# VectorE in emission order with column sums that give way, and mixing steps of TensorE joined two by two

## The chip, the cores and the metric

The kernel runs on one core of a Trainium2 chip. The metric is the device time of one execution in microseconds, the median of three runs. All engines of the core run side by side: TensorE (PE) multiplies, VectorE (DVE) and ScalarE (ACT) work element by element, GpSimd (POOL) helps, and SyncE (SP) issues nearly all transfers.

## What is computed

Two layers of a mixer over 256 latent and 256 context tokens of width 2048. Each layer norms and modulates its input, projects it with one wide matrix, runs three branches (Fourier mixing, pooling over windows, retention with 8 heads in two directions), projects each branch back, merges them with gates, and projects once more. The core of the reference:

```python
h = rms_norm(x, norm_g[l]) * (1.0 + scale) + shift          # scale, shift, gate: silu(c) @ w_ada[l] + b_ada[l]
proj = h @ w_in                                              # 2048 x 12288
y_f = (fourier_mix(f_x, w_fourier) * silu(f_g)) @ w_up_fourier
y_p = (pool_mix(p_x, w_pool, pool_scale) * silu(p_g)) @ w_up_pool
o = head_rms(retention(rope(q), rope(k), v))                 # both directions, state handed on from the context
y_r = (o * silu(r_g)) @ w_up_ret
merged = g[:, :, 0] * y_f + g[:, :, 1] * y_p + g[:, :, 2] * y_r
x = x + gate * (merged @ w_out)                              # the context likewise, in layer 0
```

In layer 1 the context only gives the retention's keys and values; its other rows are not computed.

## The kernel before

**Products.** Everything is float32. A number is split into a high and a low part, and a product takes three matmuls: high by high (L151), and the two mixed ones (L152, L153). These three lines are called the main products here. The activations are split once; the weights are split as they come.

**The stream.** The weight blocks of both layers form one list of chunks; a chunk is two 128-row tiles of a block. `stream` (L241 to L264) goes through it: for chunk i it splits chunk i+2 (ScalarE copies the high part `whi`, L206; VectorE subtracts it and leaves the low part `wlo`, L207), SyncE loads chunk i+4 (`raw`, 512 KB, L196), then TensorE multiplies chunk i. There are three `whi` and `wlo` buffers and four `raw` ones. A chunk of layer 0 is four units of six 512-column matmuls; one of layer 1 is mostly two such units.

**Background units.** The modulation matrix `w_ada` is also needed as column sums. That work is cut into units (`bg_chunk`, L438 to L473): each loads 512 KB (`bgraw`, two buffers, SyncE) and does four multiply-adds on VectorE into `bga` (L466, L468), or two where only one vector is wanted (gates of layer 1). After chunk i, five chunks in eight take one unit from the queue `bg`.

**Mixing steps.** The branches' small products (rotary embedding, transposes of heads, decays, scores, attention, Fourier, pooling) wait in the queue `mix` (`Steps`, L162 to L182). After each unit of main products the queue is told how many microseconds have passed, and lets out a step when its `after` and the `gap` of the step before are over; in layer 1 the gaps are multiplied by 0.65 from the third block on. Names that come up below: `rope_a` and `rope_b` (L590, L600: rotary embedding of a token tile, first GpSimd, then two VectorE instructions L604 and L605), `heads_T` (L679: transposes L684 of one head, ScalarE copies the result), `decayed` and `state` (L688, L696), `decays_a` (L704: two VectorE and three ScalarE instructions), `scores` (L725: matmuls L732 and a VectorE product L734), `attend` (L736), `norm_b` (L764: a reciprocal L766 and a product L767 on VectorE), `row_scale` (L1073).

**The border to the output projection.** `out_start` (L999) empties both queues before the first chunk of the output projection of a layer; in layer 0 it also splits the 16 merged tiles (`split_merged`, L996: ScalarE L431, VectorE L432). At the very end some weights are split into kept buffers (ScalarE L212, VectorE L213).

**Order.** TensorE runs in the order in which the program emits its instructions (`tc.manual_schedule` for that engine). The order on VectorE, ScalarE, GpSimd and SyncE is set by the compiler's scheduler, which may move an instruction ahead of those emitted earlier.

Of the kernel before, what the change touches and what calls it, by code (L numbers as in the profile page):

```python
# [19 lines left out]
P = 128  # L20
# [23 lines left out]
def hybrid_kernel(ctx: ExitStack, tc: tile.TileContext, a: dict, out: bass.AP):  # L44
# [196 lines left out]
    def stream(blocks):  # L241
# [17 lines left out]
        for i in range(n):  # L259
            prepare(i + 2)  # L260
            ahead(i + 4)
            chunks[i][0].products(chunks[i][1], parts.pop(i))
            if i > 5 and i % 8 in (1, 3, 5, 6, 7) and bg:
                bg.popleft()()  # L264
# [260 lines left out]
    def layer(l):  # L525
# [96 lines left out]
        class Half:  # L622


            def __init__(self, half):
# [3 lines left out]
                self.osb, self.sq = {}, {}  # L629
# [19 lines left out]
            def q_done(self, t, ps):  # L649
                self.q[t] = evac(ps)  # L650
                if t == 3:
                    for t2 in (2, 3):
                        mix.append(lambda t2=t2: rope_a(self.q, t2), gap=1.2, after=2.0)
# [7 lines left out]
            def queue_heads(self):  # L661
# [17 lines left out]
            def heads_T(self, src, tls, dst, hd):  # L679

                n = len(tls) * P
                pt = mx()
                for i, t in enumerate(tls):
                    T.transpose(pt[:, i * P:(i + 1) * P], src[t][:, hd * P:(hd + 1) * P], ident)  # L684
                dst[hd] = g()
                S.copy(dst[hd][:, 0:n], pt[:, 0:n])

            def decayed(self, d):  # L688
                self.kd = []
                for t in range(2):  # L690
# [3 lines left out]
                    self.kd.append(o)  # L694

            def state(self, d):  # L696
                ps = mx()
                for hh in range(4):
                    c = slice(hh * P, (hh + 1) * P)
                    for t in range(2):  # L700
                        T.matmul(ps[:, c], self.kd[t][:, c], self.v[t][:, c], start=t == 0, stop=t == 1)  # L701
# [97 lines left out]
        def merged_T(j, c2):  # L799

            pt = mx()
            for i in range(2):
                for t in tiles:
                    c = (2 * c2 + i) * P
# [414 lines left out]
```

## Time and profile before

| | us |
|---|---|
| median of three runs | 2446.63 (2446.52 to 2446.91) |
| the profiled execution | 2445.55 |
| its span | 2443.8 |
| TensorE busy | 2392.4 (98%) |
| VectorE busy | 1320.6 (54%) |
| ScalarE busy | 870.4 (36%) |
| GpSimd busy | 240.3 (10%) |

The profile is one execution, 1.08 us below the median. It lists how long each engine was busy, what ended each idle time, and, in the timelines, when each instruction began and how long it took. A matmul of 512 columns is shown with 0.39 us but the next one starts 0.23 us later, since they overlap; so times on TensorE are read from start to start. PEclk is the clock granted to TensorE as a share of 2.4 GHz.

### The profile page before, as it was taken

The page shows a single profiled execution, that of the slowest core. Times are in us where ns is not written, and L with a number is a line of the kernel's source. Part 1 is how long each engine was busy: PE and PEld are TensorE (multiplying, and loading weights), DVE is VectorE, ACT ScalarE, POOL GpSimd, SP SyncE. Part 2 cuts the span into 40 slices and gives each one's busy share as a digit, 9 for nine tenths or more (in the row PEclk, how much of TensorE's full clock was granted, in tenths as well). Part 3 has the DMA queues.
Part 4 walks back from the last instruction along what each step waited for, and adds up shares of the span by engine and source line. Part 5 has one row for each costly group of instructions (what it writes and reads, how often), then busy time and mean ns, then how long its engine had stood idle before and what let it go on. Part 6 is the DMA issues. An engine that isn't in the chain of part 4 may idle for free.

```text
span 2443.8 us, 28705 instructions
## 1 busy us (share of the span) xinstructions
PE 2392.4 (98%) x11288; PEld 1967.8 (81%) x11288; DVE 1320.6 (54%) x1656; ACT 870.4 (36%) x1180; POOL 240.3 (10%) x246
## 2 busy tenths in 40 slices
PE   6999999999999999999999999999999999999998
PEld 3678788778888888888888888878889888888886
DVE  4437657768256258644457432653527544545555
ACT  5222332342222232222222322563426444444444
POOL 0000200200000001110011210230302000110100
PEclk9999999999999999999999999999999999999999
DMA  9955424346345336545466343443335666676664
GB/s 338 348 170 173 138 78 148 92 136 213 115 144 187 93 119 210 156 128 169 130 202 215 112 129 112 147 150 103 100 90 146 211 191 180 181 216 183 189 204 146
DMA packets 226471, 396.58 MB, mean 162 GB/s; under 512 B 14032, under 2 KB 55376, under 8 KB 226336
## 3 DMA queue, kind: packets, MB, share of 16 engines
q1 hardware_dynamic: 221088, 379.74, 50.8%
q0 software_dynamic: 5248, 15.01, 2.1%
q8 instruction: 88, 1.44, 0.2%
q14 instruction: 47, 0.39, 0.1%
HBM read 392.60 MB, written 2.10 MB: 162 GB/s over the span
## 4 chain that ended last, share of the span: by engine, by line
PE 81%; issue 8%; DMA 5%; DVE 4%; POOL 1%; ACT 1%; SPq 0%; DVEq 0%; POOLq 0%; ACTq 0%
PE acc L151 25%; PE acc L152 25%; PE acc L153 25%; DVE bga L468 2%; DMA wa<-in_w_ada_dram 2%; DMA bgraw<-in_w_ada_dram 1%; DVE wlo L207 1%; PE mx L323 1%; PE mx L744 1%; PE mx L732 1%; PE mx L747 1%; POOL g L1085 1%; PE mx L701 0%; DMA raw<-in_w_out_dram 0%; PE mx L889 0%
## 5 line engine op out<-in xcount | busy, mean ns | idle before, releaser
L207 DVE TENSOR_TENSOR wlo<-raw,whi 128x1024 fp32r<-128x1024 f32 (+1 forms) x504 | 624.6, 1240 | 824.5 <-ACT whi L206 824.0
L206 ACT ACTIVATE whi<-raw 128x1024 fp32r<-128x1024 f32 (+1 forms) x504 | 529.2, 1050 | 1153.4 <-PE acc L153 553.5
L151 PE MATMUL acc<-whi,hm 128*128 128x512 f32 x1568 | 621.9, 397 | 0.7 <-ACT g L577 0.7
L152 PE MATMUL acc<-wlo,hm 128*128 128x512 f32 x1568 | 611.7, 390 | 2.2 <-DVE wlo L207 2.2
L153 PE MATMUL acc<-whi,hm 128*128 128x512 f32 x1568 | 611.7, 390 | 0.0
L151 PE MATMUL acc<-hm,whi 128*128 128x512 f32 (+1 forms) x1232 | 461.1, 374 | 0.7 <-ACT whi L206 0.7
L153 PE MATMUL acc<-hm,wlo 128*128 128x512 f32 (+1 forms) x1232 | 453.0, 368 | 1.0 <-DVE wlo L207 1.0
L152 PE MATMUL acc<-hm,whi 128*128 128x512 f32 (+1 forms) x1232 | 452.7, 367 | 0.0
L152 PEld LDWEIGHTS acc<-wlo,hm 128*128 128x128 f32 x1568 | 295.1, 188 | 62.7 <-DVE wlo L207 4.1
L153 PEld LDWEIGHTS acc<-whi,hm 128*128 128x128 f32 x1568 | 294.7, 188 | 62.3
L151 PEld LDWEIGHTS acc<-whi,hm 128*128 128x128 f32 x1568 | 295.0, 188 | 61.2 <-ACT g L577 1.1
L468 DVE SCALAR_TENSOR_TENSOR bga<-bgraw,sc,bga 128x512 f32<-128x512 f32 x420 | 311.8, 789 | 53.1 <-DMA bgraw<-in_w_ada_dram 51.5
L151 PEld LDWEIGHTS acc<-hm,whi 128*128 128x128 f32 x1232 | 232.6, 189 | 42.4 <-ACT whi L206 2.2
L153 PEld LDWEIGHTS acc<-hm,wlo 128*128 128x128 f32 x1232 | 232.4, 189 | 40.5 <-DVE wlo L207 2.2
L152 PEld LDWEIGHTS acc<-hm,whi 128*128 128x128 f32 x1232 | 232.6, 189 | 39.4 <-issue 1.4
L852 POOL TENSOR_TENSOR g<-g,g 128x512 f32<-128x512 f32 x32 | 52.7, 1673 | 726.5 <-DVE g L848 726.5
L151 PE MATMUL acc<-g,whi 128*128 128x512 f32 x256 | 99.7, 390 | 0.0
L152 PE MATMUL acc<-g,whi 128*128 128x512 f32 x256 | 99.6, 389 | 0.0
L153 PE MATMUL acc<-g,wlo 128*128 128x512 f32 x256 | 99.6, 389 | 0.0
L597 POOL TENSOR_TENSOR g<-g,g 128x256 f32<-128x256 f32 x32 | 29.6, 954 | 332.4 <-ACT g L577 332.4
L151 PEld LDWEIGHTS acc<-g,whi 128*128 128x128 f32 x256 | 48.1, 188 | 10.1
L152 PEld LDWEIGHTS acc<-g,whi 128*128 128x128 f32 x256 | 48.1, 188 | 10.0
(213 smaller groups left out, 1888.4 us busy)
## 6 DMA issues: line engine op xcount, KB each, us to landing
raw<-in_w_in_dram SPq DMA_DIRECT2D x368, 512.0 KB, 3.7
bgraw<-in_w_ada_dram SPq DMA_DIRECT2D x128, 512.0 KB, 4.3
raw<-in_w_out_dram SPq DMA_DIRECT2D x72, 512.0 KB, 3.6
wa<-in_w_ada_dram SPq DMA_DIRECT2D x128, 256.0 KB, 6.0
raw<-in_w_up_ret_dram SPq DMA_DIRECT2D x32, 512.0 KB, 3.8
raw<-in_w_up_fourier_dram SPq DMA_DIRECT2D x16, 512.0 KB, 3.7
raw<-in_w_up_pool_dram SPq DMA_DIRECT2D x16, 512.0 KB, 4.4
w<-in_w_in_dram SPq DMA_DIRECT2D x8, 512.0 KB, 6.6
```

What stands on the lines that cost most here:

```text
L151: T.matmul(ps, ah, bh, start=first, stop=False)
L152: T.matmul(ps, ah, bl, start=False, stop=False)
L153: at["product"] = T.matmul(ps, al, bh, start=False, stop=last)
L206: S.activation(hi[:, :, 0:w], raw[:, :, 0:w], AF.Copy)
L207: V.tensor_tensor(lo[:, :, 0:w], raw[:, :, 0:w], hi[:, :, 0:w].bitcast(F32), op=ALU.subtract)
L323: T.matmul(ps[32 * g4:32 * g4 + 32, 0:2 * n * P], sc32[:, kt, :], wa[gi, kt // rows][:, kt % rows, :, :].rearrange("p i c -> p (i c)"), st ...
L468: V.scalar_tensor_tensor(accs[ci, v], raw[:, kk, :], s, accs[ci, v], op0=ALU.mult, op1=ALU.add)
L597: G.tensor_tensor(rv[:, :, :, x, :], pv[:, :, :, 1 - x, :], sv[:, :, x, :].unsqueeze(1).to_broadcast([P, 4, 2, 32]), op=ALU.mult)
L732: T.matmul(ps[:, jt * SEQ:(jt + 1) * SEQ], self.kT[hh][:, k0:k0 + P], qs, start=True, stop=True)
L744: T.matmul(o, self.v[2 * s + jt][:, c], at[:, jt * SEQ:(jt + 1) * SEQ], start=jt == 0, stop=jt == 1 and s == 0)
L747: T.matmul(o, self.st[d][:, c], qd[:, d * SEQ:(d + 1) * SEQ], start=False, stop=d == 1)
L852: G.tensor_tensor(merged[d][:, 0:ntok], merged[d][:, 0:ntok], o[:, 0:ntok], op=ALU.add)
```

## The change

Four things change.

1. VectorE too runs in the order of emission while the stream runs (`manual_schedule` around the stream). The other three engines stay with the scheduler.
2. A background unit is taken only when fewer than two mixing steps are queued, and in three chunks of four instead of five in eight.
3. Mixing steps that have TensorE work are emitted two by two with twice the gap: transposes of two heads, both states, the attention of one head with the scores of the next, Fourier channels with positions, two pooled groups, two transposes of merged or output tiles. The two `decayed` steps now stand ahead of `rope_b`, with buffers for each direction, and the gaps after `rope_a` are doubled.
4. In layer 1 the keys' `heads_T` transposes only the latent token tiles (2, 3), not all four.

```diff
-            if i > 5 and i % 8 in (1, 3, 5, 6, 7) and bg:
+            if i > 5 and len(mix.q) < 2 and i % 4 and bg:
                 bg.popleft()()
...
                     for t2 in (2, 3):
-                        mix.append(lambda t2=t2: rope_a(self.k, t2), gap=0.8, after=2.0)
-                    mix.append(lambda: self.decayed(0), gap=1.6)
+                        mix.append(lambda t2=t2: rope_a(self.k, t2), gap=1.6, after=2.0)
+                    for d in range(2):
+                        mix.append(lambda d=d: self.decayed(d), gap=1.6)
                     for t2 in (2, 3):
                         mix.append(lambda t2=t2: rope_b(self.k, t2), gap=1.0)
-                    mix.append(lambda: (self.state(0), self.decayed(1)), gap=1.6)
-                    for hh in range(4):
-                        mix.append(lambda hh=hh: self.heads_T(self.k, (0, 1, 2, 3), self.kT, hh))
-                    mix.append(lambda: self.state(1))
+                    mix.append(lambda: (self.state(0), self.state(1)), gap=3.0)
+                    for hh in (0, 2):
+                        mix.append(lambda hh=hh: self.heads_T(self.k, tiles, self.kT, hh), gap=4.0)
...
-                    for hh in range(4):
-                        mix.append(lambda hh=hh: self.heads_T(self.q, tiles, self.qT, hh))
+                    for hh in (0, 2):
+                        mix.append(lambda hh=hh: self.heads_T(self.q, tiles, self.qT, hh), gap=4.0)
...
-                    if hh < 4:
-                        mix.append(lambda hh=hh: self.scores(hh))
-                    if hh:
-                        mix.append(lambda hh=hh: self.attend(hh - 1))
+                    mix.append(lambda hh=hh: (self.attend(hh - 1) if hh else None, self.scores(hh) if hh < 4 else None), gap=4.0)
...
-            def heads_T(self, src, tls, dst, hd):
+            def heads_T(self, src, tls, dst, h0):
...
-                        k0 = s * SEQ + jt * P
+                        k0 = s * SEQ - tok0 + jt * P
...
-                for n in range(5):
-                    if n < 4:
-                        mix.append(lambda n=n: windows(n))
-                    if n:
-                        mix.append(lambda n=n: pooled(n - 1))
+                for n in range(0, 4, 2):
+                    mix.append(lambda n=n: windows(n))
+                    mix.append(lambda n=n: windows(n + 1))
+                    mix.append(lambda n=n: (pooled(n), pooled(n + 1)), gap=3.0)
...
     run = stream(blocks0 + blocks1)
-    next(run)
-    for t in range(4):
-        halves0[0].v_done(t, v0_acc[t])
-    for i, ps in enumerate(rg_acc):
-        rg_done0(i, ps)
-    for _ in run:
-        pass
+    with tc.manual_schedule(engines={mybir.EngineType.DVE}):
+        next(run)
+        for t in range(4):
+            halves0[0].v_done(t, v0_acc[t])
+        for i, ps in enumerate(rg_acc):
+            rg_done0(i, ps)
+        for _ in run:
+            pass
```

**The order on VectorE around the queries' rotary embedding** (first half of the heads, layer 0). A row gives line, operation, output and inputs; `bga` are column sums, `wlo` the low part of a chunk's weights, and the `g` buffers on L604 and L605 are two token tiles of the queries. Before:

```order
L468 SCALAR_TENSOR_TENSOR bga_396_2206<-bgraw_467_2543,sc_87,bga_396_2206 128x512
L468 SCALAR_TENSOR_TENSOR bga_397_2208<-bgraw_467_2543,sc_87,bga_397_2208 128x512
L604 TENSOR_TENSOR g_357_1983<-g_357_1983,g_267_1379 128x512
L604 TENSOR_TENSOR g_358_1991<-g_358_1991,g_267_1379 128x512
L207 TENSOR_TENSOR wlo_361_2000<-raw_350_1923,whi_360_1999 128x1024
L605 TENSOR_TENSOR g_357_1983<-g_357_1983,g_364_2012 128x512
L605 TENSOR_TENSOR g_358_1991<-g_358_1991,g_366_2022 128x512
L468 SCALAR_TENSOR_TENSOR bga_396_2206<-bgraw_467_2543,sc_87,bga_396_2206 128x512
```

After:

```order
L468 SCALAR_TENSOR_TENSOR bga_296_1603<-bgraw_346_1909,sc_87,bga_296_1603 128x512
L207 TENSOR_TENSOR wlo_352_1952<-raw_345_1883,whi_351_1951 128x1024
L207 TENSOR_TENSOR wlo_359_1990<-raw_349_1919,whi_358_1989 128x1024
L207 TENSOR_TENSOR wlo_368_2030<-raw_353_1955,whi_367_2029 128x1024
L604 TENSOR_TENSOR g_356_1979<-g_356_1979,g_267_1381 128x512
L605 TENSOR_TENSOR g_356_1979<-g_356_1979,g_362_2002 128x512
L604 TENSOR_TENSOR g_357_1987<-g_357_1987,g_267_1381 128x512
L605 TENSOR_TENSOR g_357_1987<-g_357_1987,g_365_2019 128x512
L207 TENSOR_TENSOR wlo_375_2078<-raw_360_1993,whi_374_2077 128x1024
```

The column sums no longer stand between the tiles' instructions, and each tile's two instructions follow each other behind the `wlo` ahead of them.

**The order on VectorE at the border to the output projection of layer 0.** L848 is the last work of the third branch; L432 makes the low part of a merged tile. Before:

```order
L848 TENSOR_TENSOR g_1486_9214<-acc_1493_9246,g_1486_9214 128x512
L848 TENSOR_TENSOR g_1487_9222<-acc_1494_9253,g_1487_9222 128x512
L848 TENSOR_TENSOR g_1488_9230<-acc_1495_9260,g_1488_9230 128x512
L848 TENSOR_TENSOR g_1489_9238<-acc_1496_9267,g_1489_9238 128x512
L207 TENSOR_TENSOR wlo_1501_9313<-raw_1492_9244,whi_1500_9312 128x1024
L432 TENSOR_TENSOR hm_1546_9643<-g_725_4013,hm_1545_9642 128x512
L207 TENSOR_TENSOR wlo_1508_9347<-raw_1499_9278,whi_1507_9346 128x1024
L432 TENSOR_TENSOR hm_1548_9647<-g_726_4021,hm_1547_9646 128x512
L432 TENSOR_TENSOR hm_1550_9651<-g_727_4029,hm_1549_9650 128x512
L207 TENSOR_TENSOR wlo_1511_9377<-raw_1502_9316,whi_1510_9376 128x1024
L432 TENSOR_TENSOR hm_1552_9655<-g_728_4037,hm_1551_9654 128x512
```

After:

```order
L848 TENSOR_TENSOR g_1528_9540<-acc_1535_9572,g_1528_9540 128x512
L848 TENSOR_TENSOR g_1529_9548<-acc_1536_9579,g_1529_9548 128x512
L848 TENSOR_TENSOR g_1530_9556<-acc_1537_9586,g_1530_9556 128x512
L848 TENSOR_TENSOR g_1531_9564<-acc_1538_9593,g_1531_9564 128x512
L207 TENSOR_TENSOR wlo_1543_9639<-raw_1534_9570,whi_1542_9638 128x1024
L432 TENSOR_TENSOR hm_1546_9645<-g_701_3890,hm_1545_9644 128x512
L432 TENSOR_TENSOR hm_1548_9649<-g_702_3898,hm_1547_9648 128x512
L432 TENSOR_TENSOR hm_1550_9653<-g_703_3906,hm_1549_9652 128x512
```

Before, splits of merged tiles stand between the `wlo` of several chunks; after, all 16 stand in a row behind the fourth L848 and one more `wlo`.

**The order on VectorE in layer 1**, chunks of 2.72 us, third block on (L821 and L822 are the same gating product). Before:

```order
L821 TENSOR_TENSOR g_2248_13594<-acc_2253_13610,g_2248_13594 128x512
L821 TENSOR_TENSOR g_2249_13602<-acc_2254_13617,g_2249_13602 128x512
L207 TENSOR_TENSOR wlo_2265_13681<-raw_2260_13646,whi_2264_13680 128x1024
L207 TENSOR_TENSOR wlo_2270_13701<-raw_2263_13664,whi_2269_13700 128x1024
L207 TENSOR_TENSOR wlo_2276_13726<-raw_2266_13684,whi_2275_13725 128x1024
L207 TENSOR_TENSOR wlo_2280_13748<-raw_2271_13704,whi_2279_13747 128x1024
```

After:

```order
L822 TENSOR_TENSOR g_2249_13588<-acc_2254_13603,g_2249_13588 128x512
L207 TENSOR_TENSOR wlo_2265_13667<-raw_2260_13632,whi_2264_13666 128x1024
L207 TENSOR_TENSOR wlo_2270_13687<-raw_2263_13650,whi_2269_13686 128x1024
L466 TENSOR_SCALAR bga_2274_13708<-bgraw_2272_13704,sc_87 128x512
L468 SCALAR_TENSOR_TENSOR bga_2274_13708<-bgraw_2272_13704,sc_87,bga_2274_13708 128x512
L207 TENSOR_TENSOR wlo_2276_13712<-raw_2266_13670,whi_2275_13711 128x1024
L468 SCALAR_TENSOR_TENSOR bga_2274_13708<-bgraw_2273_13706,sc_87,bga_2274_13708 128x512 x2
L207 TENSOR_TENSOR wlo_2280_13734<-raw_2271_13690,whi_2279_13733 128x1024
L468 SCALAR_TENSOR_TENSOR bga_2274_13708<-bgraw_2278_13729,sc_87,bga_2274_13708 128x512 x2
L207 TENSOR_TENSOR wlo_2284_13756<-raw_2277_13715,whi_2283_13755 128x1024
```

Column sums for the gates of layer 1, which before had been moved up into layer 0, now stand two by two behind the `wlo` of these chunks.

## Rows read from the trace of the kernel before

**Rows 1.** the page: busy rows of TensorE and VectorE, traffic by slice, loads

```profile
PE 2392.4 (98%) x11288; PEld 1967.8 (81%) x11288; DVE 1320.6 (54%) x1656; ACT 870.4 (36%) x1180; POOL 240.3 (10%) x246
...
GB/s 338 348 170 173 138 78 148 92 136 213 115 144 187 93 119 210 156 128 169 130 202 215 112 129 112 147 150 103 100 90 146 211 191 180 181 216 183 189 204 146
...
bgraw<-in_w_ada_dram SPq DMA_DIRECT2D x128, 512.0 KB, 4.3
...
w<-in_w_in_dram SPq DMA_DIRECT2D x8, 512.0 KB, 6.6
```

**Rows 2.** waits of TensorE over the whole span (engine line <- releaser: us, times, longest)

```profile
PE mx L732 <- DVE g L734: 5.9, 1, 5.9
PE mx L684 <- DVE g L605: 5.0, 3, 4.6
...
PE acc L152 <- DVE g L213: 2.1, 3, 1.7
```

**Rows 3.** timeline of TensorE, 255 to 264 us (start, us, what, [idle before])

```profile
260.15 1.08 PE L684 MATMUL mx<-ident,g 128*128 128x128 f32 x2 [4.55 <-DVE g L605]
...
261.46 0.63 PE L152 MATMUL acc<-wlo,hm 128*128 128x512 f32 x1
261.88 0.63 PE L153 MATMUL acc<-whi,hm 128*128 128x512 f32 x1
```

**Rows 4.** windows: busy us of each engine, granted clock (PEclk), DMA share, GB/s

```profile
148.50:151.80 3.30, 3.30 (x8) 2.58 (x9) 0.65 (x1) 0.00 (x0) 0.00 (x0) 0.50 0.00 0
257.70:264.40 6.70, 4.12 (x10) 3.10 (x11) 6.70 (x10) 0.59 (x1) 0.00 (x0) 0.50 0.64 187
448.80:455.50 6.70, 3.65 (x9) 2.90 (x10) 6.70 (x10) 0.63 (x1) 1.83 (x3) 0.50 0.36 99
1960.00:2000.00 40.00, 40.00 (x178) 33.09 (x177) 19.48 (x18) 16.90 (x17) 0.00 (x0) 1.00 0.65 186
```

**Rows 5.** timeline of TensorE, 209 to 212 us

```profile
210.72 0.60 PE L684 MATMUL mx<-ident,g 128*128 128x128 f32 x4
211.08 0.47 PE L151 MATMUL acc<-whi,hm 128*128 128x512 f32 x1
211.39 0.39 PE L152 MATMUL acc<-wlo,hm 128*128 128x512 f32 x1
211.62 0.39 PE L153 MATMUL acc<-whi,hm 128*128 128x512 f32 x1
```

**Rows 6.** timeline of VectorE, 250 to 263 us

```profile
253.11 4.05 DVE L468 SCALAR_TENSOR_TENSOR bga<-bgraw,sc,bga 128x512 f32<-128x512 f32 x6
257.08 1.28 DVE L604 TENSOR_TENSOR g<-g,g 128x512 f32<-128x512 f32 x2
258.29 1.21 DVE L207 TENSOR_TENSOR wlo<-raw,whi 128x1024 fp32r<-128x1024 f32 x1
259.42 1.28 DVE L605 TENSOR_TENSOR g<-g,g 128x512 f32<-128x512 f32 x2
```

**Rows 7.** timeline of TensorE, 143 to 153 us

```profile
148.48 0.79 PE L151 MATMUL acc<-w0h,hm 128*128 128x512 f32 x1 [2.15 <-ACT hm L348]
```

**Rows 8.** timeline of TensorE, 493 to 503 us

```profile
501.08 0.50 PE L151 MATMUL acc<-hm,whi 128*128 128x512 f32 x1 [0.74 <-ACT whi L206]
```

**Rows 9.** timeline of TensorE, 1401 to 1404 us

```profile
1402.67 0.39 PE L153 MATMUL acc<-whi,hm 128*128 128x512 f32 x1
```

**Rows 10.** timeline of ScalarE, 1400 to 1406 us

```profile
1402.87 1.04 ACT L206 ACTIVATE whi<-raw 128x1024 fp32r<-128x1024 f32 x1
```

**Rows 11.** groups of VectorE by form (count | busy us, mean ns | idle before)

```profile
L468 DVE SCALAR_TENSOR_TENSOR bga<-bgraw,sc,bga 128x512 f32<-128x512 f32 x420 | 311.8, 789 | 53.1 <-DMA bgraw<-in_w_ada_dram 51.5
...
L766 DVE RECIPROCAL g<-g 128x256 f32<-128x256 f32 x8 | 13.7, 1733 | 0.6 <-ACT g L762 0.6
...
L432 DVE TENSOR_TENSOR hm<-g,hm 128x512 fp32r<-128x512 f32 x16 | 12.5, 782 | 17.1 <-PE acc L152 10.5 <-ACT hm L431 6.5
```

**Rows 12.** timeline of VectorE, the last 10 us

```profile
2437.09 0.42 DVE L1040 TENSOR_TENSOR g<-g,g 128x256 f32<-128x256 f32 x1
```

More of the change, by code (lines that the diff above doesn't have):

```diff
@@ L628, in __init__ @@
                 self.kT, self.qT, self.st, self.dec, self.at = {}, {}, {}, {}, {}
-                self.osb, self.sq = {}, {}
+                self.osb, self.sq, self.kd = {}, {}, {}
             def v_done(self, t, ps):
@@ L652, in q_done @@
                     for t2 in (2, 3):
-                        mix.append(lambda t2=t2: rope_a(self.q, t2), gap=1.2, after=2.0)
+                        mix.append(lambda t2=t2: rope_a(self.q, t2), gap=2.5, after=2.0)
                     for t2 in (2, 3):
                         mix.append(lambda t2=t2: rope_b(self.q, t2), gap=1.0)
-                    for hh in range(4):
-                        mix.append(lambda hh=hh: self.heads_T(self.q, tiles, self.qT, hh))
+                    for hh in (0, 2):
+                        mix.append(lambda hh=hh: self.heads_T(self.q, tiles, self.qT, hh), gap=4.0)
                     if not last:
@@ L677, in queue_heads @@
                     mix.append(lambda hh=hh: self.norm_b(hh))
-            def heads_T(self, src, tls, dst, hd):
+            def heads_T(self, src, tls, dst, h0):
                 n = len(tls) * P
[L682 to L686, printed above, removed]
+                for hd in (h0, h0 + 1):
+                    pt = mx()
+                    for i, t in enumerate(tls):
+                        T.transpose(pt[:, i * P:(i + 1) * P], src[t][:, hd * P:(hd + 1) * P], ident)
+                    dst[hd] = g()
+                    S.copy(dst[hd][:, 0:n], pt[:, 0:n])
             def decayed(self, d):
-                self.kd = []
+                self.kd[d] = []
                 for t in range(2):
@@ L693, in decayed @@
                                     wst[:, l, t, d, 4 * self.half:4 * self.half + 4].unsqueeze(2).to_broadcast([P, 4, P]), op=ALU.mult)
-                    self.kd.append(o)
+                    self.kd[d].append(o)
             def state(self, d):
@@ L700, in state @@
                     for t in range(2):
-                        T.matmul(ps[:, c], self.kd[t][:, c], self.v[t][:, c], start=t == 0, stop=t == 1)
+                        T.matmul(ps[:, c], self.kd[d][t][:, c], self.v[t][:, c], start=t == 0, stop=t == 1)
                 self.st[d] = evac(ps)
@@ L797, in layer, with merged_T @@
         merged, m = {}, {}
[L799 to L804, printed above, removed]
-                    T.transpose(pt[:, (2 * i + t - 2) * P:(2 * i + t - 1) * P], merged[t, j][:, c:c + P], ident)
-            for i in range(2):
-                m[4 * j + 2 * c2 + i] = split(pt[:, i * SEQ:(i + 1) * SEQ], SEQ, hmt)
+        def merged_T(j):
+            pts = []
+            for c2 in range(2):
+                pt = mx()
+                for i in range(2):
+                    for t in tiles:
+                        c = (2 * c2 + i) * P
+                        T.transpose(pt[:, (2 * i + t - 2) * P:(2 * i + t - 1) * P], merged[t, j][:, c:c + P], ident)
+                pts.append(pt)
+            for d in range(4):
+                m[4 * j + d] = split(pts[d // 2][:, (d % 2) * SEQ:(d % 2 + 1) * SEQ], SEQ, hmt)
         def token_branch(b, wname, nkt, y, first, final):
@@ L826, in up_done @@
                     if final and u:
-                        for c2 in range(2):
-                            mix.append(lambda c2=c2: merged_T(j, c2))
+                        mix.append(lambda: merged_T(j), gap=4.0)
                 if j == 1 and b == 2:
@@ L918, in fg_done @@
                 for n in range(6):
-                    if n < 4:
-                        mix.append(lambda n=n: positions(n))
-                    if 1 <= n < 5:
-                        mix.append(lambda n=n: channels(n - 1))
+                    if n < 5:
+                        mix.append(lambda n=n: (channels(n - 1) if n else None, positions(n) if n < 4 else None), gap=4.0)
                     if n > 1:
@@ L981, in pg_done @@
             if i == 3:
-                for n in range(5):
-                    if n < 4:
-                        mix.append(lambda n=n: windows(n))
-                    if n:
-                        mix.append(lambda n=n: pooled(n - 1))
+                for n in range(0, 4, 2):
+                    mix.append(lambda n=n: windows(n))
+                    mix.append(lambda n=n: windows(n + 1))
+                    mix.append(lambda n=n: (pooled(n), pooled(n + 1)), gap=3.0)
         tblock(C_PX, tiles, px_done)
@@ L1109, in done @@
                     s = t // 2
-                    for c2 in range(2):
-                        mix.append(lambda c2=c2: transposed(j, s, c2))
+                    mix.append(lambda: (transposed(j, s, 0), transposed(j, s, 1)), gap=4.0)
                     if j == 3:
```

## The prediction

> **What bounds the kernel now.** First the page: TensorE is busy 98% of the span, VectorE 54% [rows 1]. So nothing off TensorE counts unless TensorE waits for it, and all that can be won is its waits and the work it need not do. The second view is TensorE's list of waits. Behind the start-up (the first 155 us, which the change leaves alone) it is short: one wait of 5.9 us of `scores` for the score products of VectorE, waits of 5.0 us of `heads_T` for the rotary embedding, one of them 4.55 us, and small ones, among them 2.1 us for L213 at the end [rows 2, 3]. The third view, the windows, shows what else these two waits cost: during each and shortly after, the granted clock is 0.50, that is 1.2 instead of 2.4 GHz, for 6.7 us [rows 4]. At 260 us main matmuls then start 0.42 us apart [rows 3] instead of 0.23 [rows 5], seven of them (7 x 0.2 = 1.4), and the transposes and the first main one lose 0.5 more; so 1.9 us there, and by the same reckoning with four such starts 1.5 us at 453 us: 3.4 us together.
>
> Why VectorE was late is seen in its own timeline: six column sums (4.05 us) run just ahead of L604, then `wlo`, and the last L605 ends at 260.7 [rows 6]. The scheduler had put column sums ahead of work that TensorE needed next. The change takes those out of the way, so the question is what a fixed order makes late in their place.
>
> **The gains.** The sum is made against the profiled execution, 2445.55 us, which is 1.08 us under the median.
>
> - The queries' `heads_T`. In the new order nothing but `wlo` stands ahead of the four rotary instructions. They take 2.56 us [rows 6]; the gaps give TensorE about two units of 1.36 us (six starts at 0.227) between the first of them and the transposes. A `wlo` of 1.21 us can stand in front. So the wait is between 0 and 1.6 us; I take 0.8, gain 3.75.
> - `scores`. With two or more steps queued no column sum is taken, so the score product follows its `wlo` directly. I take the whole 5.9 us; if GpSimd's share of the decays is late, its 1.83 us of work there [rows 4] can stay as a wait.
> - The clock: 3.4 us, if both waits shrink to the size of those that the clock did not follow. The shortest with 0.50 granted behind it was 2.15 us [rows 4, 7]; behind the 1.7 us for L213 [rows 2] main matmuls keep the full pitch.
> - Late chunks at 494 to 502 us: three waits, 1.75 us in all, the longest on `whi` [rows 8]. With fewer sums per chunk about 0.8 stays: gain 1.0 (0 to 1.75).
> - Joining. The order shows 53 fewer switches from main products to mixing steps. What does a switch cost? Four transposes take 0.36 us from start to start, and the main matmul behind them 0.31 instead of 0.23: 0.08 is the visible loss at a switch [rows 5]. Part of it must stay, since a longer run still has one entrance and one exit, and its inner step loads weights too. I take half, 0.04: 53 x 0.04 = 2.1 us (0 to 53 x 0.085 = 4.5).
> - The keys' transposes in layer 1: 16 fewer at 0.36 / 4 = 0.09 us [rows 5]: 1.4 us. ScalarE's copies get shorter, which nobody waits for.
>
> A rule speaks against the fifth term. The Trainium skill, "TensorE: Matmul & The Clock Gate" (Architectural detail), says that TensorE's queue is a partial reorder window that pulls weight loads ahead of matmuls in flight. By that a switch would cost nothing and the joins save nothing: 2444.4 us instead of the forecast. The row with 0.31 us behind four transposes does not fully agree; no row of before shows a joined step.
>
> Gains: 3.75 + 5.9 + 3.4 + 1.0 + 2.1 + 1.4 = 17.55 us.
>
> **The losses.** VectorE now executes what is emitted first, even if it has to wait for it, and what stands behind waits too.
>
> - The border to the output projection of layer 0. Before, splits of merged tiles stood among the `wlo` of earlier chunks, and the projection's first L153 started at 1402.67 without a wait [rows 9]. Now all 16 stand behind a `wlo` whose `whi` can only be copied when chunk 215's buffer is free, at about 1402.5; before it was made at 1402.87 in 1.04 us [rows 10]. Then `wlo`, 1.21, and the first L432, at most 0.78 [rows 6, 11]: 1402.5 + 1.04 + 1.21 + 0.78 = 1405.5. TensorE needs it at 1402.67: 2.9 us. Later splits take 0.6 to 0.8 us each and are used every 0.68 us; they keep up. The wait is over 2.15 us, so I add one stretch at 1.2 GHz at 1.5 us: 4.4 (0, if the merged tiles wait less, to 4.9).
> - Layer 1, `heads_T`. Gaps are 0.65 as long, so TensorE brings only 1.4 to 2.7 us of work between `rope_b` and the transposes, against 2.56 + 1.21 us on VectorE: 1.1 to 2.4, I take 1.7.
> - Layer 1, `norm_b`. Two reciprocals of 1.73 us [rows 11] with two short products now stand between two `wlo`: 2 x 1.73 + 1.21 = 4.7 us and the products, while a chunk takes 2.72; a third follows behind the next. VectorE falls some 5 us behind (2.0, then about 1, and the products and splits) with 3 us to spare (three buffers: two chunks of 2.72 less copy and subtraction): 2.0 (0 to 4).
> - The end. In order, the addition ahead of L213 waits for ScalarE's squares once more (about 1.3 us on top of the 1.7 waited there now), and the final addition, 0.42 [rows 12], now follows the last reciprocal instead of preceding it: 1.65 (0 to 3).
> - Column sums of layer 1. Before, they were moved up into layer 0. Now 36 units stand in 50 chunks. VectorE was busy 19.5 of 40 us there [rows 4]; 72 sums at 0.789 [rows 11] are 56.8 us in 136, which makes 0.91. It holds, with little to spare: 1.0. The upper end is the first rival.
> - Three further places where the new order puts less than about 2 us of TensorE's work between what an instruction needs and its use (Fourier outputs ahead of a projection at some 2115 us, `row_scale` and a `wlo` at 1595, one evacuation at 1873). Nearest row: a late copy of 0.74 us [rows 8]; three of 0.8 make 2.5 (0 to 5).
>
> Losses: 4.4 + 1.7 + 2.0 + 1.65 + 1.0 + 2.5 = 13.25 us. `decayed`, moved ahead of `rope_b`, brings four products that read what is long there; its gaps of 1.6 cover them, and without that cover they would add their own time to the rotary wait. SyncE now issues the 36 loads of `bgraw` of layer 1 between the weights' loads; that is in the first rival. GpSimd's queue is not reordered by the change itself, and the longer gaps behind `rope_a` give it time.
>
> Net: 2445.55 - 17.55 + 13.25 = 2441.25; plus 1.08, **2442.3 us**.
>
> **Rivals.**
>
> *Column sums starve layer 1 (slower).* Loads there: 512 KB of weights in 2.72 us (193 GB/s) and 36 x 512 KB in 136 us (139): 332 GB/s. The most that a slice of the page shows is 348, at the start [rows 1]. A `bgraw` buffer is used three times in eight chunks, 7.25 us each, and holds its 1.58 us of sums and the landing. At the median of 4.3 us [rows 1] that fits. It decides at a landing of 5.65 us; at start-up, with the engines full, loads of 512 KB took 6.6 [rows 1]. At that the cycle is 8.2, 0.93 too long, for each of the 18 units that pass through one buffer: 16.7 instead of 1.0. VectorE in order then holds up `wlo` and so TensorE: 2458.0. For it: little headroom. Against it: two loads in flight should share 348 GB/s in some 3 us plus the fixed part.
>
> The Trainium skill, "DMA: Bandwidth & Descriptors" (Specifications), gives about 358 GB/s as a core's share of the memory; by that, 332 fits, which speaks against this rival. The slices at the start agree (338 and 348); no row of layer 1 comes near.
>
> *The fixed order bites nowhere but at the border (faster).* If the gaps are enough in layer 1 and at the end, only 4.4 + 1.0 is lost, and joins bring the full 4.5: 2445.55 - 19.95 + 5.4 + 1.08 = 2432.1.
>
> *The column sums give way, but the wait for the scores returns.* GpSimd and ScalarE keep their scheduled orders, and the decays pass through both; if either is late, the score products block VectorE and the 5.9 us and its 1.5 us at half clock stay: 2442.3 + 7.4 = 2449.7. The change then does not do what it says. For it: at 448 to 456 us GpSimd was busy 1.83 us in the disturbed stretch [rows 4]; against it: that is little, and the steps ahead now have longer gaps.
>
> **How the numbers follow.** A measurement can tell about 0.2% (4.9 us) from no change: below 2441.7 is faster, above 2451.5 slower. Forecast 0.55: spread by the terms' bounds between 2437 and 2448, a little over half of it below 2441.7. Faster rival 0.13, starving 0.17, returned wait 0.13 (mostly within 0.2%), the rest 0.02. Faster 0.31 + 0.13 = 0.44; the same 0.24 + 0.11 = 0.35; slower 0.17 + 0.04 = 0.21. The range leaves out half of each outer rival: 2431 to 2453.
>
> **What would show it.** Right: no wait of L684 or L732 over 1 us in layer 0, and 1.00 granted there; a wait of about 3 us of the first L153 of the projection, half clock behind it; some 130 runs of mixing steps. The starving would show as idle time of VectorE on `bgraw` between 1960 and 2120 us, and waits for `wlo` there. I am wrong if TensorE waits in layer 1 for column sums, if the border shows no wait, or if joined steps cost as much as apart.

## The result and the profile after

The changed kernel takes **2470.81 us** (median of 4 runs, 2469.42 to 2471.68) against 2446.57 before (median of four executions, the table ahead had three): a ratio of 1.0099, 95% interval 1.0081 to 1.0116. It is 24 us slower. The prediction was 2442.3 with a range of 2431 to 2453, and 0.21 for slower. The profiled execution took 2469.42 us, 23.9 more than the one of before. One execution among all that follow, in the last run of the experiments, was 13% slower at a granted clock of 0.82 and is in no median or ratio here.

The page of the kernel after, to be held against [rows 1]: TensorE's busy time is nearly the same, and VectorE has even a little less to do. The late traffic is new: up to 308 GB/s in three slices of layer 1.

```profile
PE 2396.1 (97%) x11272; PEld 1972.3 (80%) x11272; DVE 1319.4 (53%) x1656; ACT 874.0 (35%) x1183; POOL 235.6 (10%) x246
...
GB/s 338 347 162 151 71 103 107 81 139 162 166 147 174 111 137 163 158 163 143 143 157 145 120 94 121 170 111 110 78 111 117 253 308 267 176 223 179 194 195 134
...
bgraw<-in_w_ada_dram SPq DMA_DIRECT2D x128, 512.0 KB, 4.0
```

TensorE's waits behind the start-up, kernel after, in the form of [rows 2] (engine line <- releaser: us in all, times, longest):

```profile
PE acc L152 <- DVE wlo L207: 14.3, 10, 5.3
PE acc L152 <- DVE g L213: 5.2, 1, 5.2
PE acc L151 <- ACT g L572: 4.6, 1, 4.6
PE acc L153 <- DVE wlo L207: 4.1, 1, 4.1
PE acc L153 <- DVE hm L432: 3.5, 1, 3.5
PE mx L682 <- DVE g L605: 2.5, 4, 0.9
PE mx L742 <- DVE g L732: 2.4, 1, 2.4
```

The waits of before are gone: none for the score products where 5.9 us stood, and 0.65 us at the queries' transposes where 4.55 us stood (L682 is the former L684, L742 an `attend` matmul, here in layer 1). In their place stand waits of main products for VectorE. All of TensorE's waits over 0.1 us behind the start-up add up to 39.7 us, before to 19.7.

What they cost besides: windows of the kernel after, right behind three of these waits (columns as in [rows 4]; the number before the DMA share is PEclk):

```profile
519.60:522.50 2.90, 2.90 (x8) 2.25 (x8) 2.90 (x6) 0.00 (x0) 0.00 (x0) 0.50 0.88 300
...
1588.60:1594.60 6.00, 5.10 (x12) 4.03 (x13) 5.47 (x10) 2.85 (x7) 0.00 (x0) 0.51 0.55 157
...
2438.60:2441.40 2.80, 2.80 (x9) 2.15 (x8) 2.80 (x6) 0.00 (x0) 0.00 (x0) 0.58 0.55 147
```

Before, two stretches of 6.8 us had a granted clock of 0.50 [rows 4]. Now there are five of 3.4 us (behind the waits at 519, 1393, 1730, 1864 and 2438 us) and one of 6.8 (at 1590). At 1.5 us lost in each short one, as in the prediction, and twice that in the long one, they cost some 10 us instead of 3.4 (an estimate).

So the 23.9 us are: 20.0 more waiting and some 6.6 from the clock, less some 3 us. Of these 3, 1.2 are luck, since the change leaves the start-up alone: the first product with `whi` at the end of the start-up began at 154.50 instead of 155.74 us. The rest is left for fewer switches and transposes.

### The profile page after: what moved, and what is told of

It reads as the page before. It is cut to its first block, busy times and chain, and to the rows that moved or that the text cites. A ratio compares the mean times of both kernels' runs of the same rounds, so it can differ in the third digit from the quotient of the medians.

```text
span 2467.7 us, 28730 instructions
## 1 busy us (share of the span) xinstructions
PE 2396.1 (97%) x11272; PEld 1972.3 (80%) x11272; DVE 1319.4 (53%) x1656; ACT 874.0 (35%) x1183; POOL 235.6 (10%) x246
## 5 line engine op out<-in xcount | busy, mean ns | idle before, releaser
L468 DVE SCALAR_TENSOR_TENSOR bga<-bgraw,sc,bga 128x512 f32<-128x512 f32 x420 | 300.2, 766 | 6.6 <-DMA bgraw<-in_w_ada_dram 5.5
L852 POOL TENSOR_TENSOR g<-g,g 128x512 f32<-128x512 f32 x32 | 45.0, 1437 | 713.1 <-DVE g L848 713.1
L153 PEld LDWEIGHTS acc<-g,wlo 128*128 128x128 f32 x256 | 48.1, 188 | 10.0
L151 PEld LDWEIGHTS acc<-g,whi 128*128 128x128 f32 x256 | 48.1, 188 | 10.0
```

The lines of the kernel that those rows point to most:

```text
L151: T.matmul(ps, ah, bh, start=first, stop=False)
L153: at["product"] = T.matmul(ps, al, bh, start=False, stop=last)
L468: V.scalar_tensor_tensor(accs[ci, v], raw[:, kk, :], s, accs[ci, v], op0=ALU.mult, op1=ALU.add)
L852: G.tensor_tensor(merged[d][:, 0:ntok], merged[d][:, 0:ntok], o[:, 0:ntok], op=ALU.add)
```

## Where VectorE stands

The longest waits have one pattern. VectorE, kernel after, around the wait of 4.1 us at 519 us, where the retention's outputs are gated (L614), and each is split, the high part on ScalarE (L431), the low part on VectorE (L432):

```profile
504.92 0.69 DVE L432 TENSOR_TENSOR g<-g,g 128x512 fp32r<-128x512 f32 x1 [0.70 <-ACT g L431]
505.53 0.69 DVE L614 TENSOR_TENSOR g<-g,g 128x512 f32<-128x512 f32 x1
506.91 0.69 DVE L432 TENSOR_TENSOR g<-g,g 128x512 fp32r<-128x512 f32 x1 [0.70 <-ACT g L431]
507.52 1.22 DVE L207 TENSOR_TENSOR wlo<-raw,whi 128x1024 fp32r<-128x1024 f32 x1
508.66 0.69 DVE L614 TENSOR_TENSOR g<-g,g 128x512 f32<-128x512 f32 x1
...
517.44 2.35 DVE L207 TENSOR_TENSOR wlo<-raw,whi 128x1024 fp32r<-128x1024 f32 x2
```

Product, wait for ScalarE, low part, product, wait for ScalarE: each head takes 2.0 us, 0.7 of it standing still; from 503 to 517 us there are five such stands, 3.65 us together. Each L432 is emitted right behind its L614, so in a fixed order VectorE can do nothing meanwhile. The `wlo` of the next chunks are last in the line (517.44).

At 1579 to 1590 us the row sums of layer 0's output do the same, and the next `wlo` comes 8.8 us after the last one; TensorE waits 5.25 us for it. VectorE stands still four times in these 8.8 us (two are shown), 2.7 us together; the rest is its own work, which stands ahead in the line:

```profile
1579.42 1.76 DVE L207 TENSOR_TENSOR wlo<-raw,whi 128x1024 fp32r<-128x1024 f32 x1
...
1581.82 1.21 DVE L1009 TENSOR_TENSOR g<-g,g 128x512 f32<-128x512 f32 x1
1583.81 0.16 DVE L1017 TENSOR_REDUCE rs<-sst 128x1 f32<-128x4 f32 x1 [0.79 <-ACT g L1014]
...
1587.15 0.16 DVE L1017 TENSOR_REDUCE rs<-sst 128x1 f32<-128x4 f32 x1 [0.85 <-ACT g L1014]
...
1588.23 1.22 DVE L207 TENSOR_TENSOR wlo<-raw,whi 128x1024 fp32r<-128x1024 f32 x1
```

At the end a third engine joins. VectorE stands 3.85 us in front of L1037 for a square of ScalarE (L1014); ScalarE had come late to it because, in its own order, splits stood ahead whose weights had not landed. First ScalarE, kernel after:

```profile
2432.13 1.15 ACT L212 ACTIVATE hm<-raw 128x512 fp32r<-128x512 f32 x2 [2.27 <-DMA raw<-in_w_out_dram]
2433.18 0.61 ACT L1014 ACTIVATE g<-g 128x512 f32<-128x512 f32 x1
```

VectorE's row, with the releaser of its standing time at the end:

```profile
2433.92 0.69 DVE L1037 TENSOR_TENSOR g<-g,g 128x512 f32<-128x512 f32 x1 [3.85 <-ACT g L1014]
```

And it goes the other way too. In layer 1 the decays' VectorE pairs now stand behind `wlo`; ScalarE, whose instructions keep the order that the scheduler gave them, stands still for VectorE (0.62 us at 1859.76) and comes late with the silu L572 that must free a sum for TensorE, which waits 4.6 us. ScalarE, kernel after:

```profile
1858.08 1.06 ACT L206 ACTIVATE whi<-raw 128x1024 fp32r<-128x1024 f32 x1 [0.32 <-ACT g L709]
1859.76 0.63 ACT L710 ACTIVATE g<-g 128x512 f32<-128x512 f32 x1 [0.62 <-DVE g L707]
...
1863.02 1.21 ACT L572 ACTIVATE g<-acc 128x256 f32<-128x256 f32 x4
```

## Experiments

The theory after this reading: a fixed order on one engine makes it stand still for other engines in the middle of its line, with the weights' low parts queued behind. Rivals: joined steps come too late (1), column sums that give way pile up (2), VectorE has too much to do at these places (3). Every run is compared with the kernel before on the same chip, where that ran in 2442 to 2448 us, so differences of a microsecond or two are not read; "less than the whole change" goes by its ratio of 1.0099.

**Which of the parts costs the time.** First the whole change without its fixed order:

```diff
-    with tc.manual_schedule(engines={mybir.EngineType.DVE}):
-        next(run)
...
+    next(run)
...
```

> The change without its fixed order: VectorE is ordered by the scheduler again, while column sums still give way and steps are joined. Theory (the fixed order makes VectorE stand still for ScalarE with the weights' low parts queued behind): the long waits of TensorE for low parts and for L213 go, time 2439 to 2447 us. Rival 1 (joined steps come later and make TensorE wait whatever the order): the time stays at 2460 to 2470 us. Rival 2 (column sums that give way pile up later): waits for VectorE in layer 1, 2450 to 2460 us.

Measured: 2434.70 us, ratio 0.9957 (0.9942 to 0.9972), 10.6 us *faster* than before and 4 us under the expected range. Rivals 1 and 2 fall for the loss as a whole. TensorE's waits behind the start-up add up to 13.3 us, against 39.7 in the whole change. Waits of this kernel behind the start-up:

```profile
PE acc L152 <- DVE wlo L207: 6.7, 6, 3.2
PE mx L682 <- DVE g L605: 2.1, 2, 1.9
```

At the gated heads its VectorE runs three products in a row, then a `wlo`, then three low parts, without standing still:

```profile
505.13 1.89 DVE L614 TENSOR_TENSOR g<-g,g 128x512 f32<-128x512 f32 x3
506.94 1.22 DVE L207 TENSOR_TENSOR wlo<-raw,whi 128x1024 fp32r<-128x1024 f32 x1
508.07 1.88 DVE L432 TENSOR_TENSOR g<-g,g 128x512 fp32r<-128x512 f32 x3
```

Then the reverse, the kernel before with the fixed order alone:

```diff
-    next(run)
...
+    with tc.manual_schedule(engines={mybir.EngineType.DVE}):
+        next(run)
...
```

> The kernel before with nothing but the fixed order on VectorE. Theory: at least as slow as the whole change, 2465 to 2490 us, since the same chains through ScalarE stand in the order and column sums do not give way. Rival 1 (the joins cost the time): 2443 to 2449 us, as before. Rival 2: 2443 to 2449 us too.

Measured: 2497.04 us, ratio 1.0211 (1.0196 to 1.0226): 51.7 us slower, above the range. Its waits name the same releasers:

```profile
PE acc L152 <- DVE wlo L207: 18.2, 12, 5.2
PE acc L153 <- DVE wlo L207: 11.0, 5, 5.7
```

So the fixed order costs 52 us on the kernel before, and 1.0099 - 0.9957, some 35 us, beside the other parts (32 by the repeat of the first run at the end). The joins and the yield don't cause the loss as a whole; with them the fixed order costs less.

**Five places mended in the fixed order.** Each is the whole change with one place emitted otherwise; VectorE's work stays the same. The interval of each overlaps that of the whole change (1.0081 to 1.0116), so a single gain is known to some 5 us only; but the slowest execution with a mend took 2468.59 us and the fastest of the whole change 2469.42. First the gated heads: the high part comes with the product, and the low part of the head before (`held`) behind it:

```diff
                 def product():
                     V.tensor_tensor(yt[:, 0:ntok], yt[:, 0:ntok], sr[:, 0:ntok], op=ALU.mult)
...
+                    S.activation(both[0][0][:, 0:ntok], yt[:, 0:ntok], AF.Copy)
...
                 def parts():
-                    y_r[hd] = split(yt, ntok)
+                    hh, hl = both[0]
+                    V.tensor_tensor(hl[:, 0:ntok], yt[:, 0:ntok], hh[:, 0:ntok].bitcast(F32), op=ALU.subtract)
+                    y_r[hd] = hh, hl
...
+                held = mix.q.pop() if mix.q and hasattr(mix.q[-1][0], "later") else None
                 mix.append(product, gap=0.8, after=0)
+                if held:
+                    mix.q.append(held)
                 mix.append(parts, gap=0.8, after=0)
```

> The whole change, one place mended: the high part of a gated head (ScalarE) is emitted with its product, and the low part (VectorE) only behind the next head's product. VectorE has exactly the same work. Theory (VectorE stands still for ScalarE in the order): the wait of 4.1 us at 519 us goes with its half clock, and 3 to 4 of the 7.0 us of waits from 1904 to 1926 us: 8 to 10 us less than the whole change, 2459 to 2463 us. Rival (VectorE simply has too much to do there): both stay within 1 us, 2468 to 2472 us.

Measured: 2461.93 us, ratio 1.0068 (1.0051 to 1.0085), 0.0031 or 7.6 us less than the whole change; the expected 8 is just missed. The wait at 519 us is 0.65 us instead of 4.1. Some of the 7.6 lies elsewhere: the wait at the end is 3.8 us in this trace instead of 5.2, though the edit doesn't touch it. VectorE at the same place (L616 is the product, L626 the low part):

```profile
505.35 0.69 DVE L626 TENSOR_TENSOR g<-g,g 128x512 fp32r<-128x512 f32 x1
505.96 0.69 DVE L616 TENSOR_TENSOR g<-g,g 128x512 f32<-128x512 f32 x1
...
508.30 0.69 DVE L616 TENSOR_TENSOR g<-g,g 128x512 f32<-128x512 f32 x1
508.90 0.69 DVE L626 TENSOR_TENSOR g<-g,g 128x512 fp32r<-128x512 f32 x1
```

The 0.7 us gaps are gone with the work unchanged; one of 0.36 us is left at the end. Rival 3 falls for this place.

The border to the output projection:

```diff
+    if final and j == 3:
+        for d in range(0, 12, 2):
+            blocks[-1].during[d + 2] = lambda d=d: (split_merged(d), split_merged(d + 1))
...
-    for d in range(KT):
+    for d in range(12, KT):
         split_merged(d)
```

> The whole change, one place mended: 12 of 16 merged tiles are split during the last gate block, two per chunk, only four at the border to the output projection. Theory: the wait of 3.5 us at 1393 us and its half clock go, 5 us less than the whole change: 2464 to 2467 us. Rival (the border waits for the weights' low part, not for the splits): the wait stays over 2 us, 2468 to 2472 us.

Measured: 2464.27 us, ratio 1.0077 (1.0062 to 1.0092), 5.4 us less. Between 1370 and 1420 us TensorE no longer waits at all.

The row sums of layer 0:

```diff
+                def root():
                     V.tensor_reduce(r, sst[t][:, 0:q + 1], axis=AX.X, op=ALU.add)
                     S.activation(r, r, AF.Sqrt, scale=1.0 / D, bias=epst)
...
+                def inverse():
                     V.reciprocal(r, r)
...
+                    mix.append(root, gap=0.8, after=1.5)
+                    mix.append(inverse, gap=0.8)
```

> The whole change, one place mended: the row sum with its root, and the reciprocal, are steps of their own at the end of layer 0, so VectorE does not stand still for ScalarE twice per token tile. Theory: of the waits between 1557 and 1595 us (7.8 us, half clock for 6.8 us) at least 5 us and half the clock loss go: 6 to 10 us less, 2459 to 2464 us. Rival (splits and output rows are too much for VectorE there): under 2 us less.

Measured: 2463.89 us, ratio 1.0077 (1.0062 to 1.0092), 5.4 us less: below the expected 6 by a little. The wait of 5.25 us is 2.3, with the full clock behind it; another of 1.1 us came up after it. The rest there is VectorE's own work (rival 3 has a share): a split of 256 columns takes 0.92 us and `wlo` 1.76 us, see the last section.

The end:

```diff
-    V.tensor_tensor(xo, xo, fgs[j][:, c0:c0 + n], op=ALU.mult)
+    def gained():
+        V.tensor_tensor(xo, xo, fgs[j][:, c0:c0 + n], op=ALU.mult)
...
+    if j < 3:
+        mix.append(gained, gap=0.8, after=3.0)
...
```

> The whole change, one place mended: the final gain (VectorE, waits for ScalarE's squares) is a later step in the last layer's first three column blocks. Theory: the wait of 5.2 us for L213 at 2438 us shrinks to the 1.7 us of before or less, its half clock goes: 4 to 6 us less than the whole change, 2463 to 2467 us. Rival (the kept splits wait for their loads): the wait stays over 4 us, 2468 to 2472 us.

Measured: 2463.12 us, ratio 1.0070 (1.0055 to 1.0085), 7.1 us less, a little more than expected. The wait of 5.2 us for L213 is 0.2, under the 1.7 of before.

The decays of layer 1:

```diff
-    mix.append(lambda hh=hh: self.decays_a(hh), gap=1.0)
+    mix.append(lambda hh=hh: self.decays_a(hh), gap=4.0 if last else 1.0)
```

> The whole change, one place mended: the gap behind each decays_a of layer 1 is 4.0 instead of 1.0, so its VectorE pair and ScalarE exponentials come one per chunk. Theory (ScalarE, whose order is fixed too once scheduled, stands still for VectorE's decays and is late with the silu that frees a sum): the waits of 2.4 us at 1730 and 4.6 us at 1864 us fall to 3 us together or less: 4 to 8 us less than the whole change, 2463 to 2467 us. Rival (ScalarE's own work there is too much): the wait at 1864 us stays over 4 us.

Measured: 2465.04 us, ratio 1.0079 (1.0064 to 1.0094), 4.9 us less. The wait of `attend` at 1730 is gone, the one for L572 is 2.7 instead of 4.6.

All five together, and `norm_b` with a gap of 4.0:

```diff
-    mix.append(lambda hh=hh: self.norm_b(hh))
+    mix.append(lambda hh=hh: self.norm_b(hh), gap=4.0)
```

> The whole change, with five places of emission mended: high parts of the gated heads a step ahead of their low parts; 12 of the 16 merged tiles split during the last gate block instead of at the border; the root of the row sums in two steps of its own; the final gain of the last layer a step later; norm_b and decays_a of layer 1 with gaps of 4.0. Theory: the waits at 518, 1392, 1590, 1864, 1904 to 1926 and 2438 us shrink to under 1 us each with their half clocks, some 28 of 30 us of waits and 9 us of half clock: 2430 to 2440 us. Rivals 1 and 2: no more than 5 us gained, 2464 us or above.

Measured: 2437.62 us, ratio 0.9969 (0.9957 to 0.9981), so 31.8 us less than the whole change and 7.7 faster than before. The five single gains (7.6, 5.4, 5.4, 7.1, 4.9) add up to 30.4; `norm_b` was not run alone. Two waits that were to fall under 1 us did not, at the row sums (2.3) and for L572 (2.7). Waits that are left:

```profile
PE mx L696 <- DVE g L605: 3.6, 4, 1.5
PE acc L151 <- ACT g L572: 2.7, 1, 2.7
PE acc L152 <- DVE wlo L207: 2.6, 2, 2.3
```

**What the other parts are worth.** The kernel before with the joins and the 16 fewer transposes only (the column sums' old rule, the scheduler's order); against the whole change:

```diff
-    with tc.manual_schedule(engines={mybir.EngineType.DVE}):
-        next(run)
...
+    next(run)
...
-            if i > 5 and len(mix.q) < 2 and i % 4 and bg:
+            if i > 5 and i % 8 in (1, 3, 5, 6, 7) and bg:
```

> The kernel before with the joined steps and the 16 fewer transposes alone: scheduler's order, column sums in five chunks of eight. Theory: joins and transposes are worth some 3 us and the waits of before partly stay, 2438 to 2447 us. Rival 1: 2455 to 2470 us. If joins are worth 8 us (the visible tail of every step): below 2438 us.

Measured: 2439.49 us, ratio 0.9976 (0.9966 to 0.9985), 5.9 us faster. The long wait of before is not gone, it has moved by one step: `attend` waits 6.9 us for the score product. The wait for the silu L572 in layer 1 is there too:

```profile
PE acc L151 <- ACT g L572: 2.0, 1, 2.0
```

The first run, joins under the scheduler as well, has 2.1 us of it; the kernel before and the fixed order alone have none. So some 2 of the 4.6 us that TensorE waits for L572 in the whole change seem to come with the joins (rival 1), not with the fixed order.

The kernel before with the new rule for column sums only:

```diff
-    if i > 5 and i % 8 in (1, 3, 5, 6, 7) and bg:
+    if i > 5 and len(mix.q) < 2 and i % 4 and bg:
```

> The kernel before with the new rule for column sums alone: scheduler's order, steps not joined. Theory (the yield is what takes the 5.9 us wait of scores and its half clock away): 2437 to 2443 us, no wait of TensorE over 3 us in layer 0. Rival (the gain of the change without fixed order comes from joins alone): 2444 to 2449 us.

Measured: 2447.04 us, ratio 1.0005 (0.9996 to 1.0014). That expectation was wrong, and the time lies in its rival's range: alone, the yield gains nothing. The 5.9 us are gone, but three other long waits are there:

```profile
PE mx L684 <- DVE g L605: 4.0, 1, 4.0
PE acc L151 <- DVE g L848: 3.6, 1, 3.6
PE mx L486 <- ACT g L431: 2.6, 1, 2.6
```

All mends under the scheduler (the edits of the mends above and that of the first experiment together):

> All five places mended and joins and yielding sums kept, but VectorE ordered by the scheduler. Theory (the mends only undo what the fixed order did, the scheduler had no such waits): within 4 us of the change without its fixed order, 2431 to 2439 us. If the mends are worth something by themselves, for example the splits ahead of the border: under 2431 us.

Measured: 2444.84 us, ratio 0.9994 (0.9984 to 1.0003): wrong as well. The mends, worth 32 us in the fixed order, cost 7 to 9 us under the scheduler, most of it in one new wait:

```profile
PE acc L153 <- DVE hm L432: 7.2, 2, 7.0
```

The scheduler places each instruction anew when something else moves, and the long waits turn up elsewhere. So the gain of the change without its fixed order can't be split into a share of the joins and one of the yield. Whether it belongs to the program, the same kernel shows in more executions:

> The change without its fixed order once more, in more rounds. If its gain of 10 us belongs to the program: 2432 to 2438 us and a ratio of 0.994 to 0.997. If it was the spread of few executions: a ratio of 0.998 or above, like that of the joins or the yield alone.

Measured: 2437.2 us, ratio 0.9966 (0.9955 to 0.9976). It stays 8 to 11 us faster than before, and with the mended fixed order it is the fastest that ran (the two lie within 3 us); the joins alone beat both kernels too, and their 5.9 us are too near the mended order's 7.7 to be told apart.

## Why the prediction was wrong

*Right.* The two long waits of before and their half clock went: 0.65 us are left at the first queries' transposes where 0.8 was predicted, nothing at `scores`. The border to the output projection cost a wait of 3.5 us with half clock, 4.4 in all predicted; the mend gave 5.4 back. `heads_T` in layer 1 waits 0.45 and 0.93 us, 1.7 predicted; the Fourier outputs 0.8.

*The step that failed* is the pricing of the losses: 13.25 us in the sum. Its first sentence says that VectorE executes what is emitted first even if it has to wait, but the terms then add up only how long VectorE's instructions take and where they stand. How long it stands still for ScalarE between them was counted at the border and, too short, at the end alone. What the traces show in its place: VectorE's stands make up 3.65 us ahead of the wait of 4.1, 2.7 ahead of the 5.25, and 4.6 ahead of the 5.2 at the end (3.85 and 0.79). What is over is VectorE's own work that the fixed line puts ahead of the `wlo`; the mends of the border and of the decays move or spread such work. The sizes:

- Late chunks at 494 to 502 us were a gain of 1.0 in the sum; what came is a wait of 4.1 us with half clock, from the alternation of L614, L431 and L432 that [rows 8] could not show, since before it didn't exist in that order.
- `norm_b` in layer 1: 2.0 predicted, 7.0 measured (1904 to 1926 us). With the gated heads mended, waits of 2.4, 0.9 and 0.4 us remain there, so the reciprocals account for about the half, and the alternation for the rest; with the gap of 4.0 behind `norm_b` as well, 0.9 us are left in the run with all mends.
- The three tight places: 2.5 predicted. Row sums and `row_scale` alone had 7.8 us of waits between 1556 and 1590 us, the evacuation 4.6, of which some 2 seem to come with the joins.
- `attend` behind the score product in layer 1, 2.4 us, was in no term.
- The end: 1.3 us on top of the 1.7 waited before, predicted; 5.2 measured. The step "waits for ScalarE's squares once more" is right, but ScalarE's own place behind splits that wait for loads was left out.
- The clock: one stretch predicted, six came (one of them twice as long): six of the seven new waits over 2 us had one.

*Joins and transposes.* 3.5 us predicted. Eight transposes in one run, kernel after, against four in [rows 5]:

```profile
262.45 1.03 PE L682 MATMUL mx<-ident,g 128*128 128x128 f32 x8
263.24 0.48 PE L151 MATMUL acc<-whi,hm 128*128 128x512 f32 x1
263.55 0.40 PE L152 MATMUL acc<-wlo,hm 128*128 128x512 f32 x1
```

From 262.45 to 263.55 is 1.10 us, of which 0.23 is the main product's own: 0.87 for eight, against twice 0.67 - 0.23 = 0.44. By these rows a joined switch saves 0.01 us, not 0.04: joined steps cost nearly as much as apart, which the prediction had named as a sign of being wrong. 53 switches are then worth some 0.5 us, and 16 transposes at 0.11 another 1.8. The Trainium skill, "TensorE: Matmul & The Clock Gate" (Architectural detail), says that TensorE's queue can pull weight loads ahead of matmuls in flight. The rows agree with that better than my reading of [rows 5] did. Where the joins' 5.9 us in the run above come from beyond these 2 is open: its trace has 2.1 us less of waits than before (17.6 against 19.7), and the scheduler gave other places to many instructions.

*The rivals.* Column sums did not starve layer 1: no wait of TensorE from 1926 to 2116 us, loads of `bgraw` landing in 4.0 us (page after), and VectorE stands still for them 5.5 us in the whole kernel, 51.5 before [rows 11]. The three busiest slices there, 253 to 308 GB/s, stay under the 332 reckoned for the busiest chunks. None of the rivals named what happened: it was mostly the forecast's own list of losses at some three times its size (an estimate: waits, with 1.5 us for each short stretch at half clock), with the waits at 519 and 1730 us that were not on it.

What stays open: why the scheduler's order has its long waits where it has them. The order shows where an instruction stands, not why.

## What to carry to other kernels

An engine that runs in emission order pays, at every hand-over to another engine and back, the whole round trip (here 0.7 us per gated head), and everything behind it pays too. Before fixing an order, go through its line and look for pairs in which an instruction needs another engine's answer to the one just ahead; put the answer's use a step later, and add up the standing time, not the busy time. And one part at a time: here the fixed order alone cost 52 us, and the rest of the change gained 8 to 11.

## What the runs showed of the hardware

*VectorE is slower while GpSimd works.* While GpSimd scales 16 tiles (16.4 us from 1566 us on), VectorE's splits of 256 columns take 0.92 us and `wlo` 1.76; after its end 0.36 and 1.2. GpSimd in the kernel after:

```profile
1566.04 16.43 POOL L1082 TENSOR_TENSOR g<-g,g 128x256 f32<-128x256 f32 x16 [79.46 <-ACT g L1077]
```

VectorE during this and behind it:

```profile
1574.21 1.84 DVE L432 TENSOR_TENSOR hm<-g,hm 128x256 fp32r<-128x256 f32 x2
1575.98 1.76 DVE L207 TENSOR_TENSOR wlo<-raw,whi 128x1024 fp32r<-128x1024 f32 x1
...
1589.37 1.09 DVE L432 TENSOR_TENSOR hm<-g,hm 128x256 fp32r<-128x256 f32 x3
```

The Trainium skill, "GPSIMD Engine Reference" (Specifications), says that the two engines share their interface to SBUF and that VectorE instructions with two SBUF inputs contend; both of these have two, and the trace agrees. This lengthens the line ahead of the 2.3 us that the mend of the row sums left (`wlo` takes 1.76 us there too); the sum had priced `wlo` at 1.21. It is not the whole reason: the kernel before shows the same slowing (`wlo` of 1.75 us at 1578 us) and no wait over 0.52 us there.

*The clock does not follow the length of one wait alone.* In the kernel with the joins only a wait of 1.77 us at 259 us, with one of 0.27 behind it, was followed by a granted clock of 0.50, while in the change without its fixed order the full clock stayed behind a wait of 2.13 us in layer 1. The same wait of 2.44 us of `attend` in layer 1 was followed by 0.52 in the whole change (1731.6 to 1734.5 us) and by 1.00 in the run with the row sums mended (1727.2 to 1730.6). So the prediction's step from a wait over 2.15 us to one stretch at half clock holds for most waits, not for all. TensorE's timeline and a window behind it (columns as in [rows 4]), first the joins only:

```profile
258.89 0.33 PE L682 MATMUL mx<-ident,g 128*128 128x128 f32 x1 [1.77 <-DVE g L605]
```

The window behind it:

```profile
261.20:264.20 3.00, 3.00 (x8) 2.29 (x7) 3.00 (x5) 1.06 (x1) 0.00 (x0) 0.52 0.34 85
```

The change without its fixed order:

```profile
1846.57 0.39 PE L151 MATMUL acc<-hm,whi 128*128 128x256 f32 x1 [2.13 <-ACT g L572]
```

The window behind it:

```profile
1847.00:1852.00 5.00, 5.00 (x34) 4.69 (x33) 5.00 (x6) 2.12 (x5) 4.73 (x6) 1.00 0.28 94
```
